# A float32 decoder step on Trainium2: every second low part of the mixing weights made by GpSimd

## The chip, the cores and the metric

The kernel runs on one core of a Trainium2 chip. The metric is the device time of one execution in microseconds (us), as a median over runs. The engines are TensorE (PE, matrix products), VectorE (DVE), ScalarE (ACT), GpSimd (POOL) and SyncE (SP, which issues loads here). Each works through its own queue in the order in which the program was built, and waits in place when an instruction's inputs are not there.

## What is computed

The reference is one layer of a hybrid decoder for a prompt of 2048 rows (with 16 learned rows ahead of it) and 8 single-row samples, all in float32, cut here to its body:

```python
hn = rms_norm(h, norm_mix_g)
z = hn @ w_in                                   # 1024 -> 2560: u, q, f, i, g
y5 = s5_mix(u, ...)                             # diagonal complex scan, GELU, GLU (w_glu)
yh = hgrn_mix(q, f, i, g, ...)                  # 4 heads, 128x128 state, chunks of 64 rows
h = h + concatenate([y5, yh]) @ w_out
a, v = split(rms_norm(h, norm_ffn_g) @ w_up)    # 1024 -> 2 x 2816
h = h + (silu(conv3(a)) * v) @ w_down           # causal convolution of width 3
y = rms_norm(h, final_norm_g)
```

## The kernel before, in words

The prompt is cut into four blocks of 512 rows. The first phase ("mixing", to about 1195 us) does for each block the norm, the projection, the S5 part and the four heads of the HGRN part, and the output projection; the second phase is the FFN for all blocks. The two do not overlap except for a few early weight units.

A float32 product is made of three faster ones. Every operand is split into a high part (rounded to the type fp32r) and a low part, the rest: high times high, high times low and low times high (`PASS`) are summed in one PSUM bank. Weights come from memory in units of 128 x 1024 numbers. `w_unit` takes a tile `st`, has SyncE load it, and calls `split_w`: ScalarE copies `st` to the high part `wh` (L449), and VectorE subtracts `wh` from `st` to give the low part `wl` (`sub`, whose only instruction stands at L83). There are two buffers for `st` and three each for `wh` and `wl`.

In mixing the units are made in pairs or fours: a head takes four (`wf`, `wq`, and two for v and g together, which alone it loads itself and hands to `split_w`), `u_proj` four a block, `glu` two and `out_proj` eight (two for each quarter of the columns). That is 16 heads x 4 + 4 x (4 + 2 + 8) = 120 units; the FFN has 144. TensorE uses units in `fm_mm` (L480, weights stationary) and `tm_mm` (L500, weights moving); in `tm_mm` the passes of one row of weights follow each other directly, so that the low part of a unit is needed two products after its high part.

A scheduler sets the order on each queue from priorities and costs when the program is built; at run time nothing is reordered. GpSimd has few computations before the change: a power for each norm (`rstd`, L521), for which VectorE and then TensorE wait, the clearing of `att` tiles (L692), and an add for the head states (L746). It also issues the writes to memory and the gathers that go by memory: `u_d` and `udx` (L784, L783), the twelve gathers `U<-udx` a block (L793, L796), the tables of the S5 part (`tab_d`, `kt`; L358 to L442), and the results of the output projection (`h_d` at L995, `hE_d` at L1005). A head is named by block and number: head (1,0) is the first of the second block.

Of the kernel before, what the change touches and what calls it, by code (L numbers as in the profile page):

```python
# [37 lines left out]
def kernel(  # L38
# [38 lines left out]
    f_ = lambda a: a.bitcast(F32)  # L77
# [4 lines left out]
    def sub(o, a, b):  # L82
        tt_(o, a, b, op=OP.subtract)  # L83
# [185 lines left out]
    E = {}  # L269
# [8 lines left out]
    psub = lambda o, a, b: ptt(o, a, b, op=OP.subtract)  # L278
# [167 lines left out]
    def split_w(st, n):  # L446
        hi = wp.tile([128, 1024], F32R, name="wh", bufs=3)
        lo = wp.tile([128, 1024], F32R, name="wl", bufs=3)
        ACT(hi[:, :n], st[:, :n], AF.Copy)  # L449
        sub(lo[:, :n], st[:, :n], f_(hi[:, :n]))  # L450
        return hi, lo

    def w_stage():
# [2 lines left out]
    def w_unit(src, k0, nk, c0, ncol):  # L456
        st = w_stage()
        rs = src.shape[1]
        dma_w(v3(st, nk, ncol), ap(src, k0 * 128 * rs + c0, [[rs, 128], [128 * rs, nk], [1, ncol]]))
        hi, lo = split_w(st, nk * ncol)  # L460
        return v3(hi, nk, ncol), v3(lo, nk, ncol)
# [140 lines left out]
    def head(b, a, h):  # L602
# [50 lines left out]
        for kq in range(2):  # L653
            st = w_stage()
            for j in range(2):
                dma_w(st.rearrange("p (k j c) -> p k j c", k=4, j=2)[:, :, j],
                      ap(win, kq * 512 * 2560 + 1536 + 128 * h + 512 * j,
                         [[2560, 128], [128 * 2560, 4], [1, 128]]))
            hi, lo = split_w(st, 1024)
            wu.append((v3(hi, 4, 256), v3(lo, 4, 256)))  # L660
# [420 lines left out]


    ph1.close()
    pool = lambda name, bufs: ctx.enter_context(tc.tile_pool(name=name, bufs=bufs))
    gp = pool("gp", 4)
    fp = pool("fp", 2)
# [198 lines left out]
```

## Time and profile before

| what | value |
|---|---|
| median of 3 runs | 2586.27 us |
| the three runs | 2585.12, 2586.27, 2598.17 us |
| the profiled execution | 2598.71 us, of which the span (first to last instruction) is 2597.0 us |
| mean granted clock of TensorE in it | 0.982 of full speed |
| busy shares of the span | PE 95%, DVE 56%, ACT 35%, POOL 6% |
| VectorE's low parts (`wl`), whole span | 264 instructions, 318.2 us |

The profile is one execution, and that one lies 12.4 us above the median of the timed runs. A busy TensorE means that some product is running, not that it runs at its peak. "Idle before" and "waits" name the instruction whose end let the waiting engine go on. The rows behind the statements on this kernel stand in a section of their own below.

### The profile page before, as it was taken

The page shows a single profiled execution, that of the slowest core. Times are in us where ns is not written, and L with a number is a line of the kernel's source. Part 1 is how long each engine was busy: PE and PEld are TensorE (multiplying, and loading weights), DVE is VectorE, ACT ScalarE, POOL GpSimd, SP SyncE. Part 2 cuts the span into 40 slices and gives each one's busy share as a digit, 9 for nine tenths or more (in the row PEclk, how much of TensorE's full clock was granted, in tenths as well). Part 3 has the DMA queues.
Part 4 walks back from the last instruction along what each step waited for, and adds up shares of the span by engine and source line. Part 5 has one row for each costly group of instructions (what it writes and reads, how often), then busy time and mean ns, then how long its engine had stood idle before and what let it go on. Part 6 is the DMA issues. An engine that isn't in the chain of part 4 may idle for free.

```text
span 2597.0 us, 35488 instructions
## 1 busy us (share of the span) xinstructions
PE 2475.8 (95%) x14315; PEld 2149.5 (83%) x14315; DVE 1453.3 (56%) x2954; ACT 903.6 (35%) x1552; POOL 167.9 (6%) x254
## 2 busy tenths in 40 slices
PE   7896998999998999999999999999999999999998
PEld 6785876898887888898988888889888888888886
DVE  6875688668668688564343433344843333333444
ACT  3544354434434445342322222223531313131222
POOL 2232100100000000100000000000310000000000
PEclk9897999999999999999999999999999999999999
DMA  4346433544464562642111111111441111111111
GB/s 128 101 126 190 110 104 130 140 152 139 123 189 144 160 221 88 228 124 65 49 49 44 47 49 41 49 41 50 156 130 49 49 49 49 49 49 49 41 53 77
DMA packets 263658, 252.22 MB, mean 97 GB/s; under 512 B 11367, under 2 KB 233471, under 8 KB 259390
## 3 DMA queue, kind: packets, MB, share of 16 engines
q1 hardware_dynamic: 253416, 220.42, 28.1%
q0 software_dynamic: 9904, 29.48, 3.5%
q8 instruction: 112, 1.84, 0.3%
q14 instruction: 52, 0.43, 0.1%
q10 hardware_dynamic: 174, 0.06, 0.0%
HBM read 216.41 MB, written 33.27 MB: 96 GB/s over the span
## 4 chain that ended last, share of the span: by engine, by line
PE 72%; DVE 10%; issue 4%; ACT 3%; DMA 3%; POOL 1%; SPq 0%; POOLq 0%; ACTq 0%; DVEq 0%
PE mm L480 42%; PE mm L1209 9%; PE hg L1209 9%; PE mm L500 7%; DVE hf L632 1%; PE mm L514 1%; DVE wl L83 1%; DVE sB L86 1%; POOL rstd L521 1%; DVE sA L885 1%; PE tp L899 1%; DMA st<-in_w_in_dram 1%; DVE sA L86 1%; PE tp L547 1%; PE tp L847 1%
## 5 line engine op out<-in xcount | busy, mean ns | idle before, releaser
L480 PE MATMUL mm<-ah,wh 128*128 128x512 f32 (+3 forms) x2320 | 819.8, 353 | 4.5 <-ACT ah L552 3.3
L480 PE MATMUL mm<-al,wh 128*128 128x512 f32 (+3 forms) x2320 | 816.6, 352 | 1.1 <-DVE al L83 1.1
L480 PE MATMUL mm<-ah,wl 128*128 128x512 f32 (+3 forms) x2320 | 816.5, 352 | 0.5 <-DVE wl L83 0.5
L449 ACT ACTIVATE wh<-st 128x1024 fp32r<-128x1024 f32 (+1 forms) x264 | 275.7, 1046 | 731.1 <-PE mm L480 317.2
L83 DVE TENSOR_TENSOR wl<-st,wh 128x1024 fp32r<-128x1024 f32 (+1 forms) x264 | 318.2, 1206 | 345.6 <-ACT wh L449 344.0
L480 PEld LDWEIGHTS mm<-ah,wh 128*128 128x128 f32 x2320 | 442.5, 191 | 60.3 <-ACT ah L552 3.9
L480 PEld LDWEIGHTS mm<-ah,wl 128*128 128x128 f32 x2320 | 442.1, 191 | 55.9 <-DVE wl L83 1.0
L480 PEld LDWEIGHTS mm<-al,wh 128*128 128x128 f32 x2320 | 442.2, 191 | 55.2 <-DVE al L83 1.6
L500 PE MATMUL mm<-wh,ah 128*128 128x256 f32 x1024 | 294.5, 289 | 8.3 <-ACT hg L671 3.2
L500 PE MATMUL mm<-wh,al 128*128 128x256 f32 x1024 | 293.5, 287 | 5.9 <-DVE al L83 5.0
L500 PE MATMUL mm<-wl,ah 128*128 128x256 f32 x1024 | 291.6, 286 | 1.1 <-DVE wl L83 1.1
L500 PEld LDWEIGHTS mm<-wh,ah 128*128 128x128 f32 x1024 | 197.5, 193 | 11.6 <-ACT hg L671 3.4
L500 PEld LDWEIGHTS mm<-wh,al 128*128 128x128 f32 x1024 | 198.0, 193 | 8.4 <-DVE al L83 6.2
L500 PEld LDWEIGHTS mm<-wl,ah 128*128 128x128 f32 x1024 | 197.5, 193 | 1.8 <-DVE wl L83 1.5
L86 DVE TENSOR_TENSOR c<-c,mm 128x512 f32<-128x512 f32 (+1 forms) x110 | 63.8, 580 | 211.8 <-PE mm L480 210.4
L1209 PE MATMUL mm<-wh,gh 128*128 128x512 f32 x352 | 137.5, 391 | 0.0
L1209 PE MATMUL hg<-wh,gl 128*128 128x512 f32 x352 | 137.2, 390 | 0.0
L1209 PE MATMUL hg<-wl,gh 128*128 128x512 f32 x352 | 137.2, 390 | 0.0
L1209 PE MATMUL mm<-wh,gl 128*128 128x512 f32 x352 | 137.2, 390 | 0.0
L1209 PE MATMUL mm<-wl,gh 128*128 128x512 f32 x352 | 137.2, 390 | 0.0
L1209 PE MATMUL hg<-wh,gh 128*128 128x512 f32 x352 | 137.1, 389 | 0.0
L80 DVE TENSOR_TENSOR hacc<-hacc,hg 128x512 f32<-128x512 f32 x96 | 65.8, 686 | 88.2 <-PE hg L1209 87.7
(384 smaller groups left out, 3050.4 us busy)
## 6 DMA issues: line engine op xcount, KB each, us to landing
st<-in_ffn_w_up_dram SPq DMA_DIRECT2D x96, 512.0 KB
big<-tab_d SPq DMA_DIRECT2D x32, 1156.0 KB
st<-in_w_in_dram SPq DMA_DIRECT2D x48, 512.0 KB
st<-in_ffn_w_down_dram SPq DMA_DIRECT2D x40, 512.0 KB
st<-in_w_in_dram SPq DMA_DIRECT2D x64, 256.0 KB
st<-in_w_out_dram SPq DMA_DIRECT2D x32, 512.0 KB
x<-in_x_prompt_dram SPq DMA_DIRECT2D x30, 512.0 KB
h_d<-x POOLq DMA_DIRECT2D x16, 512.0 KB, 5.1
```

The source lines that it names most:

```text
L80: tt_(o, a, b, op=OP.add)
L83: tt_(o, a, b, op=OP.subtract)
L86: tt_(o, a, b, op=OP.mult)
L449: ACT(hi[:, :n], st[:, :n], AF.Copy)
L480: mm(p[:, :n], w[wi][:, k, :], a[ai][:, k, c0:c0 + n], start=(i == 0), stop=(i == 3 * nk - 1))
L500: o = mm(dst, lhs(ai, k), (hi, lo)[wi][:, kk, :], start=(i == 0), stop=(i == tot - 1))
L514: mm(dst[:m], stat[:, k, :m], w[:, kk, :], start=(i == 0), stop=(i == tot - 1))
L521: nc.gpsimd.tensor_tensor(r, r, mhalf[:ss.shape[0], :n], op=OP.pow)
L547: nc.tensor.transpose(p[:, k, :], x[:, kk * 128:kk * 128 + 128], ident)
L632: nc.vector.reciprocal(R[:, c0:c1], P[:, c0:c1])
L847: mm(pes[i // ng][:, i % ng, :], Bk[:, i, :], UT[:, i // 2, :nj], start=True, stop=True)
L1209: mm(ps_[t], gs[b, f0 + k][ai][:, t * 128:t * 128 + 128], wus[i][wi][:, kk, :], start=(k == 0 and j == 0), stop=(k == nf - 1 and j == 2))
```

## The change

The first lines add a counter to `split_w`. In mixing the low part of every unit with an even number is made by `psub`, the same subtraction on GpSimd (its instruction stands at L278 of the changed kernel); those with an odd number stay on VectorE. Before the FFN a flag is set that keeps all its units on VectorE. Since every user takes an even number of units, it is the second of each pair that moves: `wq` and the second v/g unit of each head, the second and fourth of `u_proj`, the second of `glu`, the second of each quarter of `out_proj`. That is 60 units. Nothing else is written differently, but the scheduler gives every queue a new order in mixing; from the FFN on TensorE's order is unchanged. Lines from L451 to L1083 move down by one, those behind by two.

```diff
--- before.py
+++ after.py
@@ -447,7 +447,8 @@
         hi = wp.tile([128, 1024], F32R, name="wh", bufs=3)
         lo = wp.tile([128, 1024], F32R, name="wl", bufs=3)
         ACT(hi[:, :n], st[:, :n], AF.Copy)
-        sub(lo[:, :n], st[:, :n], f_(hi[:, :n]))
+        E["nw"] = E.get("nw", 0) + 1
+        (sub if E["nw"] % 2 or "ffn" in E else psub)(lo[:, :n], st[:, :n], f_(hi[:, :n]))
         return hi, lo
 
     def w_stage():
@@ -1081,6 +1082,7 @@
 
 
     ph1.close()
+    E["ffn"] = True
     pool = lambda name, bufs: ctx.enter_context(tc.tile_pool(name=name, bufs=bufs))
     gp = pool("gp", 4)
     fp = pool("fp", 2)
```

GpSimd's queue at head (1,0) before (about 282 us); the DMAs are the last of the twelve gathers of `U` from `udx` for the S5 part of block 0:

```order
L796 DMA U_2472<-udx_162 16x16x8
L793 DMA U_2472<-udx_162 16x16x4 x3
L796 DMA U_2472<-udx_162 16x16x8
L692 MEMSET att_3576 128x512
L521 TENSOR_TENSOR rstd_3178<-rstd_3178,mhalf_124 128x4
```

The same place after; `wl_3028` is the low part of the second v/g unit of head (1,0):

```order
L794 DMA U_2472<-udx_162 16x16x4 x3
L797 DMA U_2472<-udx_162 16x16x8
L278 TENSOR_TENSOR wl_3028<-st_3024,wh_3027 128x1024
L693 MEMSET att_3576 128x512
L522 TENSOR_TENSOR rstd_3178<-rstd_3178,mhalf_124 128x4
```

The low part stands behind the last of the twelve gathers `U<-udx` and ahead of the clearing of `att`.

GpSimd's queue in the output projection of block 0 before; `h_d` takes the results of one quarter of the columns, `hE_d` those of the ten extra rows:

```order
L1005 DMA hE_d_157<-nt_5061 10x256
L995 DMA h_d0_153<-x4_5098 128x4x256
L1005 DMA hE_d_157<-nt_5201 10x256
L995 DMA h_d0_153<-x4_5238 128x4x256
L1005 DMA hE_d_157<-nt_5341 10x256
```

The same place after; `wl_5235` and `wl_5375` belong to the second units of the third and fourth quarter:

```order
L996 DMA h_d0_153<-x4_4958 128x4x256
L1006 DMA hE_d_157<-nt_5061 10x256
L996 DMA h_d0_153<-x4_5098 128x4x256
L278 TENSOR_TENSOR wl_5235<-st_5232,wh_5234 128x1024
L1006 DMA hE_d_157<-nt_5201 10x256
L996 DMA h_d0_153<-x4_5238 128x4x256
L278 TENSOR_TENSOR wl_5375<-st_5372,wh_5374 128x1024
```

Each low part now stands between the writes of the quarter before it.

GpSimd's queue at head (0,2) before, where the S5 tables are written (`tab_d`) and the samples' states are multiplied (`hn`, `nt`):

```order
L374 DMA tab_d_152<-kt__1225 128x8x256
L389 DMA tab_d_152<-big_1297 128x4x512
L389 DMA tab_d_152<-big_1314 128x4x512
L276 TENSOR_TENSOR hn_1336<-h0_1334,sv_150 128x256
L276 TENSOR_TENSOR nt_1337<-nt_1337,sv_150 128x256
L692 MEMSET att_1639 128x512
```

The same place after; `wl_1499` is the low part of the second v/g unit of head (0,2):

```order
L374 DMA tab_d_152<-kt__1225 128x8x256
L389 DMA tab_d_152<-big_1314 128x4x512
L276 TENSOR_TENSOR hn_1336<-h0_1334,sv_150 128x256
L276 TENSOR_TENSOR nt_1337<-nt_1337,sv_150 128x256
L278 TENSOR_TENSOR wl_1499<-st_1495,wh_1498 128x1024
L277 TENSOR_TENSOR hn_1336<-hn_1336,nt_1337 128x256
```

The low part has come in directly behind the write of the last table and the two products.

## Rows read from the trace of the kernel before

**Rows 1.** The page: busy time by engine, and the costliest groups.
```profile
PE 2475.8 (95%) x14315; PEld 2149.5 (83%) x14315; DVE 1453.3 (56%) x2954; ACT 903.6 (35%) x1552; POOL 167.9 (6%) x254
...
L83 DVE TENSOR_TENSOR wl<-st,wh 128x1024 fp32r<-128x1024 f32 (+1 forms) x264 | 318.2, 1206 | 345.6 <-ACT wh L449 344.0
```

**Rows 2.** Busy time in two stretches, mixing and FFN; then PEclk, DMA share, GB/s.
```profile
0.00:1195.00 1195.00, 1084.45 (x7348) 969.21 (x7349) 856.08 (x1949) 520.90 (x1005) 130.49 (x192) 0.96 0.48 143
1195.00:2597.00 1402.00, 1391.36 (x6968) 1180.26 (x6966) 597.26 (x1006) 382.68 (x548) 37.45 (x62) 1.00 0.19 58
```

**Rows 3.** Waits of TensorE in mixing: us in total, times, longest.
```profile
PE hg L726 <- DVE hg L723: 13.3, 12, 2.6
PE tp L899 <- DVE sA L83: 13.0, 15, 3.3
PE tp L547 <- DVE x L542: 10.9, 4, 7.5
PE tp L547 <- DVE rstd L520: 8.8, 2, 6.9
```

**Rows 4.** The tile `wl` on VectorE in mixing: ns min/median/max; idle before; who waited.
```profile
L83 DVE TENSOR_TENSOR wl<-st,wh x138: 1193/1222/1232, 18.0 to 1189.7; 128x1024 fp32r<-128x1024 f32 x138
...
  ACT wh L449: 111.3, 46
...
  PE mm L500: 1.1, 2
```

**Rows 5.** The chain that ended last, by line, in mixing alone.
```profile
by line: PE mm L480 17.0%; PE mm L500 14.2%; issue 8.3%; DVE hf L632 2.5%; DVE wl L83 2.2%; DVE sB L86 2.1%; DVE sA L885 1.8%; PE tp L899 1.8%; DMA st<-in_w_in_dram 1.7%; DVE sA L86 1.5%; POOL rstd L521 1.4%; PE tp L847 1.4%; DMA x<-in_x_pr
```

**Rows 6.** Groups on GpSimd in mixing: count, then busy us, mean ns, idle before.
```profile
L746 POOL TENSOR_TENSOR x<-x,fsm 128x1024 f32<-128x1024 f32 x4 | 7.7, 1913 | 10.5 <-DVE big L86 6.0 <-DMA x<-in_state_hgrn_dram 4.5
```

**Rows 7.** Timeline at 204 us, GpSimd and VectorE: start, duration, what.
```profile
204.37 1.95 POOL L746 TENSOR_TENSOR x<-x,fsm 128x1024 f32<-128x1024 f32 x1 [4.48 <-DMA x<-in_state_hgrn_dram]
...
203.87 0.69 DVE L86 TENSOR_TENSOR U<-big,U 128x512 f32<-128x512 f32 x1
...
204.68 2.19 DVE L83 TENSOR_TENSOR big<-big,U 128x512 f32<-128x512 f32 x1
```

**Rows 8.** Timeline at 1862 to 1869 us, GpSimd and VectorE.
```profile
1862.33 0.55 POOL L521 TENSOR_TENSOR rstd<-rstd,mhalf 128x1 f32<-128x1 f32 x1 [10.46 <-DVE rstd L520]
...
1865.09 4.01 POOL L521 TENSOR_TENSOR rstd<-rstd,mhalf 128x1 f32<-128x1 f32 x3
...
1866.24 2.46 DVE L1112 SCALAR_TENSOR_TENSOR hacc<-hacc,rstd,x 128x1024 f32<-128x1024 f32 x2
```

**Rows 9.** Timeline around 280 us, head (1,0): VectorE, GpSimd, TensorE.
```profile
272.43 1.23 DVE L83 TENSOR_TENSOR wl<-st,wh 128x1024 fp32r<-128x1024 f32 x1 [3.96 <-ACT wh L449]
...
282.46 1.67 POOL L793 DMA_DIRECT2D U<-udx  x3 [3.85 <-DMA U<-udx]
284.12 0.56 POOL L796 DMA_DIRECT2D U<-udx  x1
...
278.48 0.28 PE L500 MATMUL mm<-wl,ah 128*128 128x256 f32 x1
```

**Rows 10.** Busy time and clock (0.50) just behind two waits of TensorE.
```profile
448.00:461.00 13.00, 8.03 (x24) 5.96 (x24) 6.42 (x14) 4.12 (x7) 3.16 (x5) 0.50 0.33 119
```

**Rows 11.** Timeline at 515 us, output projection: GpSimd, ScalarE, VectorE, TensorE.
```profile
514.81 0.79 POOL L995 DMA_DIRECT2D h_d<-x  x1 [9.08 <-DVE Hc L892]
...
513.96 2.01 ACT L449 ACTIVATE wh<-st 128x1024 fp32r<-128x1024 f32 x2 [2.10 <-PE mm L514]
...
515.05 2.36 DVE L83 TENSOR_TENSOR wl<-st,wh 128x1024 fp32r<-128x1024 f32 x2 [0.45 <-ACT wh L449]
...
516.47 0.28 PE L500 MATMUL mm<-wl,ah 128*128 128x256 f32 x1
```

**Rows 12.** Timeline around 140 us, head (0,2): GpSimd and TensorE.
```profile
142.72 0.75 POOL L389 DMA_DIRECT2D tab_d<-big  x1 [3.05 <-ACT h L395]
...
136.93 0.28 PE L500 MATMUL mm<-wl,ah 128*128 128x256 f32 x1
```

## The prediction

> **What bounds the kernel now.** I read the busy table first: TensorE is busy for 95% of the span, VectorE for 56% [rows 1]. That mean hides two stages. In the windows by stage TensorE is idle for 10.6 us in all of the FFN, which the change leaves alone, and for 1195 - 1084.45 = 110.6 us in mixing, at a clock of 0.96 [rows 2]. So only mixing matters, and there VectorE is busy for 856 of 1195 us, 72% [rows 2]: nearly full, but not the bound. The list of waits says what those 110.6 us are. Its four longest rows all name VectorE and make 46.0 us [rows 3]: results of the recurrences and norms that come late, since their chains end there. The low parts of the weights are hardly among them. VectorE makes a `wl` in 1.22 us and is idle for 111.3 us just before these, waiting for ScalarE's `wh`; TensorE waited for one at L500 twice, for 1.1 us together [rows 4]. So the moved work is off TensorE's path today, but it stands in the queue ahead of work that is on it. The chain of waits shows how much: 2.2% of mixing, 26 us, ran through `wl`, while the power on GpSimd has 1.4% [rows 5].
>
> **What it removes.** VectorE loses 60 x 1.22 = 73.2 us [rows 4], 8.6% of its 856 us. Work behind VectorE does not shrink by that much, since most of it was covered. Lower bound: the four waits shrink as VectorE's load does, 8.6% of 46.0 = 4 us. Upper bound: half of the 26 us of the chain, 13 us, since half of the units move. I take **-8 us**, between the two, as both are readings of the same effect. Nothing at all is possible too, if each wait is a latency and no queue.
>
> **What it adds.** GpSimd gets 60 subtractions. None is in the trace there; the nearest row is the add at L746, of the same 128 x 1024 shape, at 1.91 us [rows 6]. I take this for each: 60 x 1.91 = 115 us on an engine that is busy for 130 us of mixing [rows 2]. It has room on average, so what counts is lateness and contention.
>
> *Contention.* While GpSimd ran L746 for 1.95 us at 204.37, a product of 128 x 512 on VectorE that started at 204.68 took 2.19 us; one of that shape just before took 0.69 [rows 7]. It was held until GpSimd was done. It goes the other way too: three powers on GpSimd took 4.01 us where one alone takes 0.55, while VectorE ran two 128 x 1024 instructions [rows 8]. If every moved subtraction held VectorE for its whole 1.91 us instead of the 1.22 us that it saves, VectorE would lose 60 x 0.69 = 41 us. But VectorE is idle for 28% of mixing and much of its work reads PSUM, so I expect the mean hold at some 1 us, which the saved 1.22 us still covers; it falls at other moments than the saved work, though. TensorE's four waits are 46.0 us against 856 us of VectorE's work, 5%; so 60 us of holds put 3 us on the path. I take **+2 us**, between 0 and 5.
>
> The Trainium skill has this as a rule ("SBUF — State Buffer", section "Who interferes with whom"): a VectorE instruction with two inputs in SBUF contends with a GpSimd instruction that reads SBUF, and the one that comes second waits for the whole of the first. It speaks against this change, since the moved subtraction reads SBUF and the recurrences are of that kind; the trace agrees with 2.19 against 0.69 us. By the rule alone the moved work would only slow VectorE, and the sum would be that of the second rival below. On the price, "GPSIMD Engine Reference", section "Performance versus the Vector engine", has 4497 ns for twice the elements, an estimate of 2.25 us here; the 1.91 us of the trace stands instead, and 2.25 would add 20 us to GpSimd's queue.
>
> *Lateness.* The queue on GpSimd holds issues of DMAs that wait. I followed each moved unit: when its `wh` ends, what stands ahead of it on GpSimd in the new order and when that ran in the trace, plus 1.91 us, against TensorE's first product with it. Most have 4 to 30 us to spare. Three places have not.
>
> Head (1,0): `wl` was made on VectorE at 272.43 and is wanted by TensorE at 278.48. Now it stands behind all twelve gathers `U<-udx`, of which the last four wait 3.85 us for a transfer and the last is issued at 284.12 for 0.56 us [rows 9]. So it is there at 284.68 + 1.91 = 286.6, and TensorE, which is in order, stands still for 286.6 - 278.5 = **8.1 us**. After long waits the clock has fallen: in the 13 us behind waits of 3.3 and 4.5 us the granted clock was 0.50, the lower level of 1.2 GHz, with 8.0 us of busy time [rows 10], which at full clock is 4 us of work. So half of a stretch of this kind is lost; since some of it would be waiting anyway I take **+3 us**, in all +11. The bounds are 0, if the gathers come sooner, and 13.
>
> Output projection: `tm_mm` wants the second unit 4 x 3 products after the first. At 513.96 ScalarE makes two `wh` (2.01 us, to 515.97), and VectorE two `wl` from 515.05 (2.36 us, to 517.41, the first one done at 516.3); TensorE took the second unit's at 516.47 [rows 11]. In the new order this unit waits for GpSimd's issue of `h_d`, 514.81 + 0.79 = 515.6, and is done at 517.5, **1.0 us** late. This is the worst of the 16 pairs of this place; seven more, and one in head (1,1), have less than 0.8 us to spare or are late by the same comparison. Half a microsecond for each of these nine is **+5 us** (rounded; bounds 2.5 and 8: some 0.3 and 0.9 each).
>
> Head (0,2): the low part stands behind the write of the last table. That was issued at 142.72 for 0.75 us, TensorE wants the low part at 136.93 [rows 12], so at the old times it would come some 10 us late. But the transposes and copies that feed those tables stand earlier on TensorE and ScalarE in the new order as well. I take **+2 us**, between 0 and 10.
>
> **Sum.** -8 + 2 + 11 + 5 + 2 = +12 us on the profiled execution's 2598.71, so 2610.7. That execution lies 12.4 us above the median of 2586.27, so I put the same difference on the median: **2598 us**, 0.5% slower. About 0.5% is what a measurement of this kernel can tell from no change; it is 2573 to 2599 us for "the same", so the forecast lies at its edge.
>
> **The rivals.** First, *the chain gains and the queue does not block*: the gathers finish sooner since VectorE is ahead, so the 11 us and most of the 7 us are not there, and the half of the chain is won in full, with the clock held where waits vanish: -13 to -20, about **2570 us**. For it: 2.2% of the chain [rows 5], and 72% load on VectorE. Against: twelve gathers that wait for DMA stay ahead whatever VectorE does [rows 9].
>
> Second, *the shared port decides*, the slower side: each moved subtraction is held itself by what VectorE runs, as the powers were [rows 8], and lasts not 1.91 but 3 us or more. The nine tight units then each come 1.1 to 2.4 us later (3.0 to 4.3 us in place of 1.91), which is +10 to +22, besides the +12 or most of it. It decides as soon as the mean on GpSimd passes some 3 us. That gives about **2612 us**. For it: VectorE is 72% busy, much of it with two inputs in SBUF. Against: GpSimd is only blocked where VectorE was first.
>
> Third, *nothing happens*: `wl` was off TensorE's path [rows 4] and stays so, freed time and stalls cancel: **2586 us**.
>
> **Chances.** Forecast (2588 to 2608) 0.42; the shared port 0.28; the gain 0.15; nothing 0.15. The forecast's half above 2599 and most of the port's case make slower by over 0.5% 0.45; the gain below 2573 makes faster 0.15; the rest, 0.40, is within. The range leaves out most of the gain's case and the upper end of the port's: 2574 to 2618.
>
> **What would show it.** VectorE's busy time in mixing should fall from 856 to some 800 us; if it falls by less than 40 us, the holds are greater than I took. The moved subtractions should last 1.9 us at the median, and if their mean passes 3 us, the port has it. TensorE should wait for a `wl` made by GpSimd at L501 for 5 to 10 us in head (1,0), right behind the last `U<-udx`, and in the output projection some eight times for under 1.5 us. If the list of waits has no `wl` from GpSimd with more than 5 us in all, the lateness term was wrong and the time should come out under 2590. The four rows of [rows 3] should fall by 4 to 13 us together; if they grow, freeing VectorE was worth nothing. The FFN should stay within 2 us; if not, I have overlooked something in the second phase.

## The result

The changed kernel takes **2681.35 us** (median of 4 runs, 2675.12 to 2684.99) against 2589.68 us for the kernel before in the same runs: a ratio of 1.0345, 95% interval 1.0320 to 1.0369, or 92 us more. The forecast was 2598 us with a range to 2618. The direction was right; the size was not: +92 us where +12 was forecast.

The profiled execution of the changed kernel took 2675.12 us, near its median. The one of the kernel before that the prediction started from, 2598.71 us, lies some 9 us above the median of all its runs here (2590 us), so the sizes below go by the timed medians where they can.

The page of the changed kernel: busy time by engine, then the two groups of low parts (count, busy us, mean ns, idle before):

```profile
PE 2497.0 (93%) x14315; PEld 2168.7 (81%) x14315; DVE 1468.1 (55%) x2894; ACT 902.7 (34%) x1552; POOL 317.0 (12%) x314
...
L83 DVE TENSOR_TENSOR wl<-st,wh 128x1024 fp32r<-128x1024 f32 x204 | 256.3, 1257 | 314.3 <-ACT wh L449 313.5
...
L278 POOL TENSOR_TENSOR wl<-st,wh 128x1024 fp32r<-128x1024 f32 x60 | 150.8, 2514 | 465.9 <-ACT wh L449 389.7
```

The windows of mixing, which now ends at 1271.4 us (the first product of the FFN behind the 7349 of mixing), and of the FFN; busy us of PE, PEld, DVE, ACT, POOL with counts, then PEclk, DMA share, GB/s:

```profile
0.00:1271.40 1271.40, 1105.55 (x7349) 988.72 (x7350) 871.23 (x1889) 520.03 (x1005) 279.59 (x252) 0.95 0.44 135
1271.40:2673.40 1402.00, 1391.46 (x6968) 1179.98 (x6966) 596.88 (x1006) 382.66 (x548) 37.41 (x62) 1.00 0.19 58
```

The FFN is what it was (its window here runs to the end of the span; from its first product to TensorE's last it takes 1391 us in this kernel as in the one before). Mixing is 76 us longer than in the profile of [rows 2]. VectorE lost 60 low parts of 1.22 us, 73 us, and yet its busy time in mixing has *risen* from 856 to 871 us: 88 us have come in that no instruction asked for. TensorE was idle for 166 us in place of 111, and needed 1105.6 us for the products that took 1084.4 before: 55 of the 76 us are waiting, 21 are slower products.

TensorE's waits in mixing now (us in total, times, longest):

```profile
PE tp L900 <- DVE sA L83: 31.5, 19, 3.0
PE hg L727 <- DVE hg L724: 16.8, 15, 5.5
PE mm L501 <- POOL wl L278: 14.8, 9, 8.3
PE tp L815 <- DVE sY L808: 10.9, 6, 4.8
PE tp L548 <- DVE x L543: 8.8, 6, 4.5
PE tp L548 <- DVE rstd L521: 8.4, 2, 6.3
```

Against [rows 3] the waits for the scans of the S5 part (`tp <- sA`) have gone from 13.0 to 31.5 us, those for `hg` from 13.3 to 16.8, and low parts from GpSimd are new with 14.8. The tile `wl` on GpSimd: ns min/median/max, and the weight loads that waited for it:

```profile
L278 POOL TENSOR_TENSOR wl<-st,wh x60: 2337/2389/2922, 23.3 to 1158.9; 128x1024 fp32r<-128x1024 f32 x60
...
  PEld mm L501: 16.6, 9
```

The subtraction lasts 2.39 us there, not the 1.91 us of the row that the prediction took [rows 6].

### The profile page after: what moved, and what is told of

It is laid out like the page before. It is cut to its first block, busy times and chain, and to the rows that moved or that the text cites. A ratio compares the mean times of both kernels' runs of the same rounds, so it can differ in the third digit from the quotient of the medians.

```text
span 2673.4 us, 35525 instructions
## 1 busy us (share of the span) xinstructions
PE 2497.0 (93%) x14315; PEld 2168.7 (81%) x14315; DVE 1468.1 (55%) x2894; ACT 902.7 (34%) x1552; POOL 317.0 (12%) x314
## 4 chain that ended last, share of the span: by engine, by line
PE 56%; DVE 2%; DMA 1%; POOL 1%; ACT 1%; issue 0%; POOLq 0%; ACTq 0%; SPq 0%; DVEq 0%
PE mm L481 36%; PE mm L1211 9%; PE hg L1211 9%; PE mm L501 1%; DMA st<-in_w_out_dram 1%; PE mm L515 1%; DMA x<-h_d 0%; PE tp L548 0%; DVE hacc L1114 0%; POOL rstd L522 0%; POOL wl L278 0%; DVE x L543 0%; ACT wh L449 0%; DVE sA L886 0%; ACT al L531 0%
## 5 line engine op out<-in xcount | busy, mean ns | idle before, releaser
L481 PE MATMUL mm<-ah,wh 128*128 128x512 f32 (+3 forms) x2320 | 821.5, 354 | 5.6 <-ACT ah L553 3.9
L481 PE MATMUL mm<-al,wh 128*128 128x512 f32 (+3 forms) x2320 | 819.9, 353 | 0.7 <-DVE al L83 0.7
L481 PE MATMUL mm<-ah,wl 128*128 128x512 f32 (+3 forms) x2320 | 817.6, 352 | 1.8 <-POOL wl L278 1.8
L481 PEld LDWEIGHTS mm<-ah,wh 128*128 128x128 f32 x2320 | 444.4, 192 | 61.8 <-ACT ah L553 4.5
L481 PEld LDWEIGHTS mm<-ah,wl 128*128 128x128 f32 x2320 | 443.6, 191 | 56.5 <-POOL wl L278 2.2
L481 PEld LDWEIGHTS mm<-al,wh 128*128 128x128 f32 x2320 | 443.8, 191 | 55.1 <-issue 1.8
L83 DVE TENSOR_TENSOR wl<-st,wh 128x1024 fp32r<-128x1024 f32 x204 | 256.3, 1257 | 314.3 <-ACT wh L449 313.5
L501 PE MATMUL mm<-wl,ah 128*128 128x256 f32 x1024 | 295.3, 289 | 16.5 <-POOL wl L278 14.8
L501 PE MATMUL mm<-wh,ah 128*128 128x256 f32 x1024 | 295.7, 289 | 9.6 <-ACT hg L672 5.5
L501 PE MATMUL mm<-wh,al 128*128 128x256 f32 x1024 | 296.2, 290 | 6.1 <-DVE al L83 3.8
L501 PEld LDWEIGHTS mm<-wl,ah 128*128 128x128 f32 x1024 | 199.8, 195 | 19.6 <-POOL wl L278 16.6
L501 PEld LDWEIGHTS mm<-wh,ah 128*128 128x128 f32 x1024 | 200.2, 196 | 11.6 <-ACT hg L672 5.7
L501 PEld LDWEIGHTS mm<-wh,al 128*128 128x128 f32 x1024 | 200.2, 196 | 9.9 <-DVE al L83 5.0
L278 POOL TENSOR_TENSOR wl<-st,wh 128x1024 fp32r<-128x1024 f32 x60 | 150.8, 2514 | 465.9 <-ACT wh L449 389.7
```

Of the source, the lines that this page charges most:

```text
L481: mm(p[:, :n], w[wi][:, k, :], a[ai][:, k, c0:c0 + n], start=(i == 0), stop=(i == 3 * nk - 1))
L501: o = mm(dst, lhs(ai, k), (hi, lo)[wi][:, kk, :], start=(i == 0), stop=(i == tot - 1))
```

## One hold, followed to its end

Head (2,1), by timelines of ScalarE, GpSimd, VectorE and TensorE (start, duration, what):

```profile
630.84 1.06 ACT L449 ACTIVATE wh<-st 128x1024 fp32r<-128x1024 f32 x1 [0.79 <-PE mm L481]
...
632.04 2.90 POOL L278 TENSOR_TENSOR wl<-st,wh 128x1024 fp32r<-128x1024 f32 x1 [5.81 <-ACT wh L449]
...
631.64 0.48 DVE L886 TENSOR_TENSOR_SCAN sA<-sv,Hc,sB 128x128 f32<-128x128 f32 x1
632.04 0.67 DVE L83 TENSOR_TENSOR sA<-sA,sB 128x516 f32<-128x516 f32 x1
632.63 2.60 DVE L886 TENSOR_TENSOR_SCAN sA<-sv,Hc,sB 128x128 f32<-128x128 f32 x1
...
635.20 0.85 DVE L886 TENSOR_TENSOR_SCAN sA<-sv,Hc,sB 128x128 f32<-128x128 f32 x2
...
639.66 0.14 DVE L893 COPY Hc<-sA 128x4 f32<-128x4 f32 x1
...
639.60 1.22 PE L900 MATMUL tp<-big,sA 128*128 128x128 f32 x4 [2.62 <-DVE sA L83]
```

ScalarE has the high part ready at 631.90, and GpSimd starts its subtraction at 632.04. VectorE's scan at L886 has two inputs in SBUF; the one at 631.64 takes 0.48 us, the next of the same shape, at 632.63, takes 2.60 us and ends just after GpSimd is done at 634.94. GpSimd, too, is longer here (2.90 us against a median of 2.39), which fits VectorE's 128 x 516 subtraction that began at the same 632.04. The 2.1 us are never won back: the scans, the copies and the rotation behind them follow one another without a gap, and TensorE, which had nothing else next in its order, waits 2.62 us for `sA` until 639.60. Then comes a second price, the clock. Windows of three microseconds around that wait:

```profile
637.00:640.00 3.00, 0.41 (x2) 0.41 (x3) 3.00 (x11) 0.80 (x2) 0.00 (x0) 0.92 1.06 394
640.00:643.00 3.00, 3.00 (x13) 2.81 (x13) 2.97 (x4) 0.39 (x1) 0.00 (x0) 0.51 0.26 111
643.00:646.00 3.00, 3.00 (x26) 2.96 (x26) 3.00 (x6) 1.06 (x1) 0.00 (x0) 1.00 0.92 324
```

In the first three microseconds after the wait TensorE is busy throughout at a granted clock of 0.51, the lower level of 1.2 GHz; in the next three it is at 1.00. (The counts of products, 13 and 26, do not show the price by themselves, since the products differ in size.) Three busy microseconds at half the clock do 1.5 us of work, so by this estimate 1.5 us more are gone. Such waits for `sA` come back head after head: 12 of the 19 last 1.9 to 3.0 us. With the clock behind them they are a good part of what the heads lose (some 3 us each: 61 us less the 12 to 14 of one stall, both below, over 16 heads).

**All holds together.** For each instruction of VectorE in mixing, its duration can be compared with the median of its form in the kernel before. The 128 that overlap a GpSimd subtraction are 81 us longer than these medians; the 1761 others are 10.5 us longer, about as the instructions of the kernel before itself are (9.5 us over the same medians). So VectorE's excess stands beside GpSimd's subtractions. Of the 128, 48 carry all of it, 2.0 us each at the median: a hold mostly strikes one instruction, for most of the 2.4 us. And 12 of the 48, with 23 of the 81 us, have a single tensor input: they are scalings, a cast and copies, such as this one of 128 x 4 (GpSimd, then VectorE):

```profile
358.50 2.45 POOL L278 TENSOR_TENSOR wl<-st,wh 128x1024 fp32r<-128x1024 f32 x1 [18.77 <-ACT wh L449]
...
358.75 2.22 DVE L893 COPY Hc<-sA 128x4 f32<-128x4 f32 x1
```

The 32 copies of this line took 0.14 to 0.17 us before.

```profile
L892 DVE COPY Hc<-sA x32: 142/153/170, 317.6 to 1004.9; 128x4 f32<-128x4 f32 x32
```

## The experiments

The theory after this reading (**port**): GpSimd's subtraction and VectorE's two-input instructions shut each other out while both read SBUF, and TensorE pays. The rivals: **queue** (GpSimd is in order, so low parts, powers and DMA issues come late), and **order** (the scheduler's new order of mixing is itself worse). Changes are against the changed kernel's line in `split_w`:

```
(sub if E["nw"] % 2 or "ffn" in E else psub)(lo[:, :n], st[:, :n], f_(hi[:, :n]))
```

**GpSimd's work almost without reading SBUF.**

```diff
-  psub(lo[:, :n], st[:, :n], f_(hi[:, :n]))
+  psub(lo[:, 0:2], st[:, 0:2], f_(hi[:, 0:2]))
+  nc.gpsimd.memset(f_(lo[:, 2:n]), 0.0)        # twice
```

> The low parts of the 60 moved units are not computed: GpSimd subtracts two columns (so that it waits for the same inputs at the same place of its queue) and clears the rest of the tile twice, which takes its time but reads no SBUF. Port theory (the 92 us come from GpSimd and VectorE blocking each other while both read SBUF): VectorE's busy time in mixing falls from 871 to below 800 us, the repeated 2.6 us waits at the transposes of sA go, and the time falls to 2585 to 2605. Queue theory (the units, powers and DMA issues come late because GpSimd is in order): the waits stay, 2650 to 2680. Order theory (the scheduler's new order of mixing is itself bad): also 2650 to 2680, with VectorE's busy time low.

Measured: 2596.26 us, ratio 1.0025 (1.0016 to 1.0035). Mixing of this kernel, columns as above:

```profile
0.00:1192.40 1192.40, 1085.12 (x7349) 973.11 (x7350) 797.43 (x1889) 520.51 (x1005) 260.81 (x372) 0.96 0.47 144
```

VectorE is busy for 797 us, 15 us above the 783 that its own work makes (856 - 73), and TensorE's waits for `sA` and `hg` are these:

```profile
PE hg L727 <- DVE hg L724: 13.0, 15, 3.1
PE tp L900 <- DVE sA L83: 8.5, 19, 0.8
...
PE mm L501 <- POOL wl L451: 7.2, 1, 7.2
```

The 31.5 us for `sA` have become 8.5, none longer than 0.8 us. GpSimd is busy for 261 us, still twice the 130 us of before, and 60 instructions of its queue still want `wh`; yet 85 of the 92 us are gone. They are not all the port's. The scheduler put one or both clears of most units ahead of the two-column subtraction, so that a low part is there 1.3 us after its `wh` at the median, in place of 2.6 in the changed kernel. TensorE's waits for low parts fell from 16.6 us (14.8 above, and 1.8 at L481) to the 7.2 of head (1,0). Without these 9 us, some 76 us are left for the port; 76 to 85 is the estimate. TensorE's order is nearer to that of the changed kernel (it differs at 835 of the 7349 places of mixing) than to that of the kernel before (2296); that the time is within 6 us of before all the same speaks against the order theory.

**The port alone, with nobody waiting for GpSimd's results.** In the first two kernels VectorE makes all low parts, and GpSimd in addition subtracts into a scratch tile (832 columns), or as a control clears that tile; in the third the tile has 768 columns.

```diff
+  sub(lo[:, :n], st[:, :n], f_(hi[:, :n]))                       # every unit
+  psub(du, st[:, :832], f_(hi[:, :832]))                         # every second one, du: 832 columns, bf16
+  psub(du[:, 0:2], st[:, 0:2], f_(hi[:, 0:2])); nc.gpsimd.memset(du[:, 2:], 0.0)   # the control: the clear three times
```

> All low parts are made by VectorE as in the kernel before; in mixing GpSimd in addition subtracts 832 columns of every second unit into a scratch tile that nobody reads. Nobody waits for GpSimd's work and VectorE's order is nearly that of before. Port theory: VectorE is held for some 50 to 75 us in all, busy 910 to 930 us in mixing, and the time grows by 50 to 90 us, to 2640 to 2680. Queue theory: only the powers and DMA issues behind the subtractions can be late, 2590 to 2615. Order theory: as before, 2580 to 2600.

> The control of the run before: the same 60 additions to GpSimd's queue, but each subtracts two columns and clears the scratch tile three times, so hardly reads SBUF. All low parts are made by VectorE. Port theory: within 15 us of the kernel before, 2575 to 2605. Queue theory: as much as with the added subtractions. Order theory: 2580 to 2600.

> As the run with added subtractions of 832 columns, but of 768, so that the scratch tile is 1536 bytes in a partition in place of 1664. That run and its control lost 29 us in the FFN, where nothing was changed but the addresses of the tiles. If the addresses do that: FFN back to 1392 us and the time 2645 to 2660, the port's part alone. If anything else that the added tile brings: again 2680 to 2690.

Measured: 2688.70 us for the added subtractions (1.0382, 1.0364 to 1.0400), 2631.22 for the control (1.0157, 1.0140 to 1.0174), 2656.60 for 768 columns (1.0248, 1.0229 to 1.0267). The first lies above what the port theory gave, and the control agrees with no theory; the third lies where it was expected. The windows of the control, mixing and FFN:

```profile
0.00:1194.60 1194.60, 1081.63 (x7348) 964.34 (x7349) 863.33 (x1949) 521.11 (x1005) 328.79 (x432) 0.97 0.47 143
```

```profile
1194.60:2615.60 1421.00, 1420.37 (x6968) 1179.87 (x6966) 594.46 (x1002) 381.84 (x546) 36.33 (x60) 1.00 0.18 56
```

Its mixing is as long as that in the profile of before (which lies 9 us above its median); most of the loss is in the FFN, 1420.8 us from its first product to TensorE's last in place of 1391.4, where the change does nothing. The run with 832 columns has 1420.6 us there, the one with 768 columns 1391.5. So the fair pair is 768 columns against the control without its 29.4 us in the FFN: 2656.6 against 2601.8, **55 us for the port alone**, while queue and scratch tile cost 12 us against 2590. The pair is not alike in everything: the tiles differ in size, and three clears of 0.79 us stand for one subtraction, which lasts 1.80 to 5.43 us (2.76 at the median) and wants the same `wh` as VectorE's own low part. Mixing with 768 columns:

```profile
0.00:1252.90 1252.90, 1100.91 (x7349) 982.85 (x7350) 923.57 (x1949) 521.39 (x1005) 278.09 (x252) 0.95 0.45 137
```

VectorE is busy for 923.6 us, 67.5 more than before and 60.2 more than in the control, with the same instructions. And they come in the same order: TensorE's differs from that of the kernel before at 23 of the 7349 places of mixing, VectorE's at 21 of 1949. So 65 us of loss come without a new order, and the order theory is out as the main cause.

**One unit given back.** The second v/g unit of head (1,0) is the 24th.

```diff
-(sub if E["nw"] % 2 or "ffn" in E else psub)(...)
+(sub if E["nw"] % 2 or E["nw"] == 24 or "ffn" in E else psub)(...)
```

> The changed kernel with one unit given back to VectorE: the second v/g unit of head (1,0), which stood behind the twelve gathers U<-udx. TensorE's order is the same. Prediction's lateness term: 8 us of waiting and some 2 us of half clock go, 2669 to 2673. If TensorE's later waits take up the gain: no change, 2679 to 2683.

Measured: 2666.88 us (1.0298, 1.0279 to 1.0317), 14.5 us less than the changed kernel by the medians and 12 by the ratios, so a little more than the 8 to 12 expected; TensorE's order is the same. In the changed kernel the place reads (GpSimd, then TensorE):

```profile
295.59 0.56 POOL L794 DMA_DIRECT2D U<-udx  x1 [3.88 <-DMA U<-udx]
296.56 1.11 POOL L794 DMA_DIRECT2D U<-udx  x2 [0.41 <-DMA U<-udx]
297.66 0.56 POOL L797 DMA_DIRECT2D U<-udx  x1
298.24 2.35 POOL L278 TENSOR_TENSOR wl<-st,wh 128x1024 fp32r<-128x1024 f32 x1
...
300.64 0.58 PE L501 MATMUL mm<-wl,ah 128*128 128x256 f32 x1 [8.26 <-POOL wl L278]
```

The low part starts when the last gather `U<-udx` has been issued, and TensorE waits 8.26 us. The wait is as long as predicted (8.1 us); what makes the rest, the clock after it or the work of that head, was not taken apart.

**The clears, with that unit given back.** The edit is the sum of the two above.

> The run with clears in place of subtractions (low parts of 59 units are not computed), with the unit behind the twelve gathers given back to VectorE. It shows what the freed time of VectorE is worth when neither the port nor that stall takes it back. Prediction's term: -8 us (between -4 and -13) against the kernel before, some late low parts of the output projection included: 2577 to 2586. If VectorE's freed time is worth nothing: 2588 to 2595.

Measured: 2585.25 us, ratio 0.9985 (0.9974 to 0.9996), 11 us less than with the clears alone. This is VectorE's freed time with little of the port and without that stall: worth 4 us by the ratio (1 to 7), 6.5 by the medians, so at the low end of the prediction's term. VectorE is busy for 798 us of mixing there, so 58 us are freed and not 73: the clears still hold it for 15.

**Shorter pieces.**

```diff
-  psub(lo[:, :n], st[:, :n], f_(hi[:, :n]))
+  [psub(lo[:, j:j + 256], st[:, j:j + 256], f_(hi[:, j:j + 256])) for j in range(0, n, 256)]
```

> The changed kernel with each of GpSimd's 60 subtractions cut into four of 256 columns, same values. Port theory with the length of a hold as what counts: GpSimd lets go of the port after each piece, so that no instruction of VectorE is held for more than some 0.8 us in place of 2.4; the 2.6 us waits at the transposes of sA become under 1 us and the time falls to 2610 to 2650, though each low part takes 3 us or more on GpSimd. If the sum of the holds is what counts: 2670 to 2700, since the bytes read are the same and VectorE's busy time in mixing stays near 871 us. Queue theory: the low parts are later than before, 2680 to 2710.

Measured: 2663.68 us (1.0281, 1.0265 to 1.0296), between the two: 18 us better. A piece on GpSimd, ns min/median/max, and mixing:

```profile
L278 POOL TENSOR_TENSOR wl<-st,wh x240: 712/738/2920, 23.4 to 1150.0; 128x256 fp32r<-128x256 f32 x120
```

```profile
0.00:1260.70 1260.70, 1106.70 (x7349) 989.52 (x7350) 850.97 (x1889) 521.70 (x1005) 345.32 (x432) 0.95 0.45 136
```

Pieces of 0.74 us took VectorE's excess from 88 to 851 - 783 = 68 us, and the time fell with it, by 18 us. One hold is shorter (0.53 us at the median), but the pieces strike one after another. The place of head (2,1) shown above reads here (GpSimd, then VectorE):

```profile
620.39 3.56 POOL L278 TENSOR_TENSOR wl<-st,wh 128x256 fp32r<-128x256 f32 x4 [5.82 <-ACT wh L449]
...
620.97 0.96 DVE L886 TENSOR_TENSOR_SCAN sA<-sv,Hc,sB 128x128 f32<-128x128 f32 x1
621.85 0.62 DVE L893 COPY Hc<-sA 128x4 f32<-128x4 f32 x1
622.39 1.85 DVE L886 TENSOR_TENSOR_SCAN sA<-sv,Hc,sB 128x128 f32<-128x128 f32 x2
```

The scan, the copy and the two scans take 3.4 us in place of the 1.5 of free ones (0.48, 0.14 and 0.85), again some 2 us, and TensorE still waits 18 times for `sA`, 23.6 us in all and up to 2.9. So it is the sum of the holds that counts more than the length of one. None of the three expectations held.

**Where the units are.** A flag set in `head` chooses the units.

```diff
+(psub if E["nw"] % 2 == 0 and E.get("hd") else sub)(...)                       # heads alone, 32 units
+(sub if E["nw"] % 2 or E.get("hd") or "ffn" in E else psub)(...)               # the others, 28 units
```

> GpSimd makes the low parts of the second units of the heads alone (32), VectorE all others. Port theory: most of the loss, since the recurrences of S5 and the heads run on VectorE at that time; read from the times at which TensorE begins each unit, the heads lost some 58 of the 76 us of mixing: 2640 to 2660. Queue theory (output projection with no spare time): most of the loss is elsewhere, 2605 to 2620 (the stall at head (1,0) remains).

> The complement: GpSimd makes the low parts of the second units of u_proj, glu and out_proj alone (28), VectorE all those of the heads. Port theory: 18 of the 76 us, 2600 to 2615. Queue theory: the late low parts of the output projection cost more than half, 2630 to 2650. If the two parts add up, this run's loss and that of the heads alone make 92 us.

Measured: heads alone 2651.95 us (1.0236, 1.0219 to 1.0253), the others 2620.62 (1.0112, 1.0097 to 1.0127). Mixing of the two:

```profile
0.00:1248.70 1248.70, 1102.05 (x7348) 987.31 (x7349) 867.87 (x1917) 519.90 (x1005) 209.01 (x224) 0.95 0.45 137
```

```profile
0.00:1216.80 1216.80, 1092.03 (x7348) 974.15 (x7349) 858.90 (x1921) 520.83 (x1005) 200.35 (x220) 0.96 0.47 141
```

Their losses, 61 and 29 us, make 90 of the 92. By VectorE's excess, 868 - (856 - 32 x 1.22) = 51 us and 859 - (856 - 28 x 1.22) = 37 us, the sum is again 88. The heads alone lie where the port theory had them; the others lie between the two expectations, 6 us above the port's. A unit in a head costs 1.9 us with the stall at head (1,0) and some 1.5 without it, one elsewhere 1.0.

**VectorE's time without the port.**

```diff
-  psub(du, st[:, :768], f_(hi[:, :768]))
+  sub(du, st[:, :768], f_(hi[:, :768]))
```

> The run with 768 added columns, with the added subtraction made by VectorE itself in place of GpSimd: some 1 us each, 60 us more work in VectorE's queue directly behind the low part, and no port to share. If TensorE pays for VectorE's time wherever it falls: as much as the 67 us of holds cost, 2640 to 2655. If what counts is that a hold falls on moments in which VectorE has work, while the low parts fall mostly where it waits for ScalarE: 2595 to 2615.

Measured: 2622.59 us (1.0120, 1.0096 to 1.0144), 33 us more, which neither expectation holds. Mixing:

```profile
0.00:1219.40 1219.40, 1086.62 (x7349) 968.62 (x7350) 907.07 (x2009) 520.04 (x1005) 132.66 (x192) 0.96 0.47 141
```

51 us more on VectorE (907 - 856) cost 33 us (25 to 37), so 0.64 us for each; 67.5 us of holds cost 65 us against before, and 60.2 cost 55 against the control, so 0.9 to 1.0 each. As a hold, then, a microsecond of VectorE is dearer. How dear added work is by itself is not shown: this kernel's order is another (TensorE's differs from that of before at 2035 of 7349 places), which may have a part in the 33 us.

**A kernel that might beat both.**

```diff
-            nc.gpsimd.tensor_tensor(s0v, s0v, fsm[...], op=OP.mult)
+            nc.vector.tensor_tensor(s0v, s0v, fsm[...], op=OP.mult)
```

> The kernel before with its only four wide computations on GpSimd, the products of head states of 128 x 1024 (L746, 1.9 us each), given to VectorE. Port theory: 5 us of holds go at 0.9 us each, 4 x 1.2 us of VectorE's time cost little: 2583 to 2588, 2 to 6 us under the kernel before, so faster than both kernels. If VectorE's time costs as much as a hold: no change, 2588 to 2593.

Measured: 2593.93 us, ratio 1.0010 (0.9999 to 1.0021): no gain, and just above both expectations. VectorE is busy for 855 us of mixing, as before, with 4 x 1.22 us more of its own work: the four products had held it for about what it needs to make them itself. No kernel that computes everything came out below the kernel before.

**The addresses.** Against the kernel before, ahead of the first tile of the weights' pool:

```diff
+    nc.gpsimd.memset(wp.tile([128, 832], mybir.dt.bfloat16, name="du", bufs=1), 0.0)
```

> The kernel before with nothing added but one unused tile of 1664 bytes in the pool of the weights (cleared once at the start), which moves the addresses of the tiles allocated behind it. If addresses alone slow TensorE's products in the FFN: FFN 1421 us in place of 1392 and the time 2612 to 2625. If the 29 us came from the repeated work on the tile: 2585 to 2595.

Measured: 2594.02 us (1.0011, 0.9998 to 1.0025), with the FFN at 1391.4 us. The tile alone, allocated ahead of the others of its pool, does nothing; what the 29 us of the control are is left open (last section).

## Why the prediction went wrong

**The step that failed** is the contention term, +2 us, where the run with clears gives 76 to 85. It had three parts. The duration: 1.91 us from the nearest row [rows 6]; measured 2.39. That row is no add but a product with an operand repeated along the row; the moved subtraction reads two full tiles. The Trainium skill ("GPSIMD Engine Reference", section "Performance versus the Vector engine") would have given an estimate of 2.25 us, which is nearer; the measurement decides for 2.39. The hold: "some 1 us" for each unit; measured 88 us of excess over 60 units, 1.5 us each, more than the 1.22 us saved. Both are off by a quarter to a half and make little. The third part was the conversion: four waits of TensorE were 46 us of VectorE's 856, 5%, so 60 us of holds were to cost 3 us. Measured, a microsecond of hold cost 0.9 to 1.0 us. That is where nearly all of the missing 80 us are.

The ratio of waits to work says what share of VectorE's time TensorE waited for; it does not say what one more microsecond costs. VectorE was busy for 72% of mixing on average [rows 2], but a hold can only fall on a moment in which it has something to run. At head (2,1) the chain of scans and rotations follows on there without a gap, with TensorE's order behind it; that it is so at the other holds is inferred from the waits for `sA` that return.

**The freed time** was rightly small: -8 us predicted, -4 (-7 to -1) measured once most of the port and the stall were out of the way. [rows 4] gives a reason: 46 of the 138 low parts lay behind a wait for ScalarE, 111 us in all, and TensorE hardly waited for any. So what was taken off was cheap time, and what was put on was dear time; the sum of VectorE's busy time shows neither.

**Head (1,0)** was right: 8.26 us of waiting against 8.1, 11.0 to 14.5 us in all against 11. **The tight units** of the output projection were about right: the waits for GpSimd's low parts at L501 apart from head (1,0) are 14.8 - 8.3 = 6.5 us in 8 waits of 0.4 to 1.1 us, all of them there, where 5 us were put. Head (0,2), for which 2 us were put, has no wait for its low part; one of 1.8 us at L481, in another head, was not foreseen.

**The second rival** named the port and had its direction, but not its path: it let GpSimd's subtraction grow past 3 us and charged the late low parts. The subtraction grew to 2.9 us at most, 2.51 in the mean, so the sign of that rival, a mean above 3 us, did not come; what paid was VectorE. With the 88 us of holds at one microsecond each the sum would have been 88 - 8 + 11 + 7 = 98 us, close to the 92 measured; a hold of full length, as [rows 7] shows it, was the row to start from. The rule of the Trainium skill ("SBUF — State Buffer", section "Who interferes with whom") had said the same: VectorE's two-input instructions are shut out by a GpSimd instruction that reads SBUF, for the whole of it. The 2.60 against 0.48 us above agree, and so do the clears, which hardly read and leave 15 of the 88 us. The prediction quoted the rule and then discounted it by the 5%. The holds went beyond two-input instructions, though: 23 of the 81 us above.

**What was to be seen:** VectorE's busy time in mixing was to fall by 40 us or more; it rose by 15, which was named as the sign of greater holds. The four waits of [rows 3] were to fall; together they grew from 46.0 to 65.5 us (31.5 + 16.8 + 8.8 + 8.4). The FFN stayed, as said.

What is not settled: why 58 us less on VectorE are worth 4 us and 51 us more cost 33. The place in the queue (some of the freed low parts lay beside a wait, an added one stands directly ahead of a chain) would do it, but the scheduler gave these two kernels orders of their own, and no run makes either change in the order of the kernel before.

## What to carry to other kernels

Before wide two-input work goes to GpSimd, look at what VectorE runs at the moment when that work becomes ready: if VectorE is busy with instructions that read two SBUF operands, or with copies and scalings from SBUF to SBUF, count up to the full duration on GpSimd as lost on VectorE (here 88 of GpSimd's 151 us), and price it at what VectorE's tightest chain costs (here 0.9 to 1.0 us for each microsecond of hold), not at VectorE's mean load or at the share of waits. VectorE's busy time in the stage, against the sum of its own instructions, is the reading that shows it after the fact. And a DMA issue that waits on GpSimd's queue is a wait for any computation behind it: that part can be read off the order and the trace to the microsecond.

## What the runs showed of the hardware

The loss of 29 us in the FFN of the control was not expected. Rows of one group of products in the FFN, the control first, then the run with 768 columns (count, busy us, mean ns):

```profile
L1211 PE MATMUL hg<-wh,gl 128*128 128x512 f32 x352 | 139.2, 395 | 0.0
```

```profile
L1211 PE MATMUL hg<-wh,gl 128*128 128x512 f32 x352 | 137.2, 390 | 0.0
```

The same products took 395 ns in place of 390 at a granted clock of 1.00 in both; over all of the FFN the loss is 29.4 of 1391.4 us, 2.1%. The scratch tile was 1664 bytes a partition in the one and 1536 in the other, which moves the tiles allocated behind it. The order is not the cause: the runs with 832 and 768 columns have TensorE's products in the same order from first to last, and only the first loses the 29 us. That addresses are the cause fits, but the run with a tile of 1664 bytes ahead of the weights' own tiles did not show it, so a shift of weights and activations together does nothing; whether it is the distance between the weights' tiles and those of the activations was not tried.

The clears on GpSimd hardly held VectorE's scans, and yet 15 us of excess stayed with 60 pairs of clears. By the medians of before, most of what the instructions beside GpSimd's clears and two-column subtractions lost there (17 of 22 us) fell on copies and scalings with one tensor input, such as the copies of 128 x 4 from SBUF to SBUF at L883 (0.15 us at the least, 1.05 at the most), where before none took more than 0.24.
